# Attention's units 2.05 instead of 1.65 weight blocks apart among the long products of a two-layer hybrid trunk

## The chip, the cores and the metric

The kernel runs on one core of one Trainium2 chip. The metric is the device time of one execution in microseconds, median of the runs. A core has five engines with a queue of instructions each: TensorE (PE in the profile, its weight loads PEld), VectorE (DVE), ScalarE (ACT), GpSimd (POOL) and SyncE (SP, which here only issues transfers). TensorE writes its results to PSUM, of which the kernel uses eight banks of 128 x 512 fp32; VectorE and ScalarE read them out.

## The reference, cut to what matters

Two layers, 512 tokens, model width 1024, fp32. Each layer normalises x, projects it with one wide matrix, runs two branches on parts of the result, merges them under two gates, projects back, and then runs a squared-ReLU MLP of width 4096:

```python
z = rmsnorm(x, norm_mix) @ w_in      # q | k | v | q_m | k_m | v_m | o_m | i/f | gate A | gate B
att = sliding_window_attention(rope(rmsnorm(q)), rope(rmsnorm(k)), v, sinks)   # 8 heads, 2 kv heads of 64
hm  = rmsnorm(mlstm_chunkwise(q_m, k_m, v_m, i, f)) * sigmoid(o_m)             # 4 heads
x = x + (sigmoid(gA) * (att @ w_att_branch) + sigmoid(gB) * (hm @ w_m_branch)) @ w_out
x = x + relu(rmsnorm(x) @ w_ff1)**2 @ w_ff2
```

Attention works on four blocks of 128 queries; each sees its own block and the one before, within 128 positions:

```python
scores = where(valid, q_blk @ [k_prev, k_blk].T / 8, -inf)
m = max(scores.max(-1), sink); p = exp(scores - m)
out = (p / (p.sum(-1) + exp(sink - m))) @ [v_prev, v_blk]
```

## The kernel before, in words

**Products.** Every fp32 weight and activation is split into a high and a low part that TensorE multiplies faster; a product of two split operands is three matmuls (`mm3`). A long product takes weight blocks of 128 x 512: a block is loaded (SP), split by one ScalarE copy (L192) and one VectorE subtraction (L193), and multiplied in four steps of three matmuls each. A step counts as 0.25, so one **weight block** is 1.0 on the scale by which everything here is placed. The results of four steps lie in four PSUM banks until VectorE or ScalarE reads them out (`ev_...`); three pairs of banks, x, y and f, are used in turn by the long products.

**The list of a mixer.** `weave` (L255) takes the steps of the long products in order and a list `side` of other work, each piece with a place on that scale, and emits a piece as soon as the products have reached its place. The products of the second `weave` in a mixer, with the blocks they span: mLSTM q and k 0 to 8, gate products 0 and 1 from 8 to 24, mLSTM v (`ev_v`) 24 to 32, attention's branch product `a_steps` in two halves 32 to 40, gate product 2 to 48, output gate to 56, gate product 3 to 64.

**Emission is not the order on the engines.** The framework orders each engine's instructions once, when the program is built: the earlier an instruction was emitted, the sooner its turn, but one whose inputs, bank or tile are not there yet by its own model of times gives way to later ones that are ready. What stands under `tc.high_priority()` (weight splits, read-outs of the long products) goes ahead. On the chip each engine then works through its fixed order, waiting where something is late. So the profile can show a piece several blocks behind its place.

**Attention, in eight units.** Unit (b, kv) is a block of queries and a kv head, with i = 2 b + kv from 0 to 7. Its steps and what they cost the engines:

- `k_tr(b)` and `q_tr(b)`, once per block: transposes by TensorE into one bank each; k is read out by four ScalarE copies (L593, L594) and four VectorE operations (L595, L596), q by four pairs of a ScalarE copy (L615) and a VectorE operation (L616) that take turns on the bank.
- `att_scores`, twice: matmuls of q with the keys (tile names `aux<-kT,t`) into one bank; ScalarE copies the earlier block's half (L638), VectorE the masked half (L639, `copy_predicated`), which frees the bank.
- `att_softmax`: VectorE maximum (L646, L647), four ScalarE exponentials (L652), VectorE sums and scaling (L655 to L657).
- `att_probs`: four transposes (`aux<-ident,t`), a split by ScalarE (L204) and VectorE (L205), two GpSimd masks (L671, L673).
- `att_out`: two or four matmuls with v (`aux<-t,v`), then ScalarE and VectorE read-outs (L685, L689) and a split (L692, L693) into the tiles that the branch product multiplies.

All these results, and those of the gating and the mLSTM, go through `aux()`, a pool of two PSUM banks. The pool `act` has 24 tiles of 128 x 512 and the pool `tmp` 18.

**Beside attention** stand in the same list `gating0` to `gating3` (small VectorE and ScalarE work for the mLSTM gates, with a few aux matmuls) at 8.45 and every 3 blocks on, and `qk_split` n = 0 to 7 (L709 on), which splits the mLSTM's queries and keys per head: one ScalarE copy (L713), one VectorE subtraction (L718 or L721), for queries a GpSimd copy and memset too. The mLSTM's own heads begin at 28 (`m_decay`), their weights at 29.75.

Places before, in weight blocks: unit i starts at 7 + 1.65 i with its first scores, second scores and softmax 1.25 later, probabilities at + 3.45, output at + 5.65. `q_tr(b+1)` and `k_tr(b+1)` stand 1.75 and 1.25 ahead of the first unit of that block. The splits stand at 9.6 + 1.65 n.

Of the kernel before, what the change touches and what calls it, by code (L numbers as in the profile page):

```python
# [35 lines left out]
def hybrid_kernel(ctx, tc, x, norm_mix, w_in, att_q_norm, att_k_norm, att_sinks, m_gate_bias,  # L36
# [36 lines left out]
    def slot(dt=F32, shape=(P, T)):  # L73
        return now["act"].tile(list(shape), dt, tag="a", name=nm("a"))

    def temp(dt=F32):
        return now["tmp"].tile([P, T], dt, tag="t", name=nm("t"))
# [10 lines left out]
    def aux(shape=(P, T)):  # L88
        return paux.tile(list(shape), F32, tag="aux", name=nm("aux"))
# [4 lines left out]
    def f32(ap):  # L94
        return ap.bitcast(F32)
# [331 lines left out]
    def mixer(l, norm, late, order, phase):  # L427
# [153 lines left out]
        def k_vec(b):  # L581
            rope(kvi[:, b, 0:128].rearrange("p (h d) -> p h d", d=HD), b, HKV)

        def k_tr(b):

            ps = aux([P, P])
            pe.transpose(ps, kvi[:, b, 0:128], ident)
            for h in range(HKV):
                r = slice(64 * h, 64 * h + 64)
                o = slice(64 - 64 * h, 128 - 64 * h)  # L590
                c = slice((b + 1) * P, (b + 2) * P)
                g = gcols[1][r, l:l + 1]
                sc.activation(kTh[r, h, c], ps[r, :], AF.Copy, scale=g)  # L593
                sc.activation(kTh[o, h, c], ps[r, :], AF.Copy, scale=g)  # L594
                ve.scalar_tensor_tensor(kTl[r, h, c], ps[r, :], g, f32(kTh[r, h, c]), op0=ALU.mult, op1=ALU.subtract)  # L595
                ve.tensor_copy(kTl[o, h, c], f32(kTl[r, h, c]))  # L596

        def q_vec(b):
            rope(q_tok[b].rearrange("p (h d) -> p h d", d=HD), b, HQ)

        def q_tr(b):


            ps = aux()
            for j in range(4):
                pe.transpose(ps[:, j * P:(j + 1) * P], q_tok[b][:, j * P:(j + 1) * P], ident)
            for j in range(2):
                qT[b, j] = temp(F32R)
                t4 = qT[b, j].rearrange("p (n i t) -> p n i t", n=2, i=2)
                p4 = ps[:, 2 * j * P:2 * (j + 1) * P].rearrange("p (n t) -> p n t", n=2)  # L610
                for i in range(2):
                    r = slice(64 * i, 64 * i + 64)
                    o = slice(64 - 64 * i, 128 - 64 * i)
                    g = gcols[0][r, l:l + 1]
                    sc.activation(t4[r, :, i, :], p4[r], AF.Copy, scale=g)  # L615
                    ve.scalar_tensor_tensor(t4[o, :, i, :], p4[r], g, f32(t4[r, :, i, :]), op0=ALU.mult,  # L616
                                            op1=ALU.subtract)

        def att_scores(b, kv, hp):
            if hp == 0:  # L620
                sps[b, kv] = temp()
            ps = aux()
            for i in range(2):
                c = 2 * hp + i
                lhs = qT[b, kv][:, c * P:(c + 1) * P]
                o = ps[:, i * 2 * P:(i + 1) * 2 * P]
                ks = slice(b * P, (b + 2) * P)
                if b == 0:

                    o, ks = o[:, P:], slice(P, 2 * P)  # L630
                pe.matmul(o, lhs, kTh[:, kv, ks], start=True, stop=False)
                pe.matmul(o, lhs, kTl[:, kv, ks], start=False, stop=True)
            p4 = ps.rearrange("p (h w k) -> p h w k", h=2, w=2)
            dst = sps[b, kv][:, hp * 2 * P:(hp + 1) * 2 * P].rearrange("p (h k) -> p h k", h=2)
            if b == 0:
                gp.memset(dst, NEG)
            else:
                sc.activation(dst, p4[:, :, 0, :], AF.Copy)  # L638
            ve.copy_predicated(dst, tri_i.unsqueeze(1).to_broadcast([P, 2, P]), p4[:, :, 1, :])  # L639

        def att_softmax(b, kv):
            sp = sps[b, kv]
            s3 = sp.rearrange("p (h k) -> p h k", h=4)
            hs = slice(4 * kv, 4 * kv + 4)
            m = sm([P, 4], "m")
            ve.tensor_reduce(m, s3, axis=AX.X, op=ALU.max)  # L646
            ve.scalar_tensor_tensor(m, m, -1.0, nsinks[:, l, hs], op0=ALU.mult, op1=ALU.min)  # L647
            es = sm([P, 4], "es")
            ve.tensor_tensor(es, sinks[:, l, hs], m, op=ALU.add)
            den = sm([P, 4], "den")  # L650
            for i in range(4):
                sc.activation(s3[:, i, :], s3[:, i, :], AF.Exp, bias=m[:, i:i + 1],  # L652
                              accum_out=den[:, i:i + 1])
            sc.activation(es, es, AF.Exp)
            ve.tensor_tensor(den, den, es, op=ALU.add)  # L655
            ve.reciprocal(den, den)
            ve.tensor_tensor(s3, s3, den.unsqueeze(2).to_broadcast([P, 4, P]), op=ALU.mult)  # L657

        def att_probs(b, kv):
            sp = sps[b, kv]  # L660
            pt = aux()
            for i in range(4):
                pe.transpose(pt[:, i * P:(i + 1) * P], sp[:, i * P:(i + 1) * P], ident)
            hl = split(pt, get=lambda: temp(F32R))
            parts[b, kv] = [(hl, b)]
            if b > 0:

                prev = [temp(F32R) for _ in hl]
                for src, dst in zip(hl, prev):
                    s3, d3 = (t.rearrange("p (h q) -> p h q", h=4) for t in (src, dst))  # L670
                    gp.affine_select(out=d3, in_=s3, compare_op=ALU.is_gt, fill=0.0, base=0,  # L671
                                     pattern=[[0, 4], [-1, P]], channel_multiplier=1)
                    gp.affine_select(out=s3, in_=s3, compare_op=ALU.is_ge, fill=0.0, base=0,  # L673
                                     pattern=[[0, 4], [1, P]], channel_multiplier=-1)
                parts[b, kv].append((prev, b - 1))
# [33 lines left out]
        def qk_split(m, i):  # L709
            t = qk_raw[m]  # L710
            r, o = slice(64 * i, 64 * i + 64), slice(64 - 64 * i, 128 - 64 * i)
            d = slot(F32R)
            sc.activation(d[r], t[r], AF.Copy)  # L713
            if m < 2:
                gp.tensor_copy(d[o], f32(d[r]))
                low = slot(F32R)
                gp.memset(f32(low[o]), 0.0)
                ve.tensor_tensor(low[r], t[r], f32(d[r]), op=ALU.subtract)  # L718
                m_q[2 * m + i], m_ql[2 * m + i] = d, low
            else:  # L720
                ve.tensor_tensor(d[o], t[r], f32(d[r]), op=ALU.subtract)  # L721
                m_k[2 * (m - 2) + i] = d
# [11 lines left out]
        def gate_steps(g, then=lambda: None):  # L734
            sg = []

            def ev(m, ps):
                sg.append(slot())
                ve.tensor_tensor(sg[m], ps, row[0], op=ALU.mult)
                if m == 3:  # L740
                    then()

            return sg, feat_steps(acts, wcols(C_G + 512 * g, 512), ev)
# [3 lines left out]
        def ev_v(b, ps):  # L747
            if b == 0:
# [6 lines left out]
        side = [(0, lambda: k_vec(0)), (0, lambda: q_vec(0)), (0, lambda: k_vec(1)), (0, lambda: q_vec(1)),  # L755
                (7 - 1.25, lambda: k_tr(0)), (7 - 1.75, lambda: q_tr(0))]
        for i, (b, kv) in enumerate(units):
            at = 7 + 1.65 * i
            side += [(at, lambda b=b, kv=kv: att_scores(b, kv, 0)),
                     (at + 1.25, lambda b=b, kv=kv: att_scores(b, kv, 1)),  # L760
                     (at + 1.25, lambda b=b, kv=kv: att_softmax(b, kv)),
                     (at + 3.45, lambda b=b, kv=kv: att_probs(b, kv)),
                     (at + 3.45 + 2.2, lambda b=b, kv=kv: att_out(b, kv))]
            if kv == 0 and b + 1 < NB:
                if b + 2 < NB:
                    side += [(at + 1, lambda b=b: k_vec(b + 2)), (at + 1, lambda b=b: q_vec(b + 2))]
                side += [(at + 2 * 1.65 - 1.25, lambda b=b: k_tr(b + 1)), (at + 2 * 1.65 - 1.75, lambda b=b: q_tr(b + 1))]
        side += [(8.45 + 3.0 * i, f) for i, f in enumerate((gating0, gating1, gating2, gating3))]
        side += [(9.6 + 1.65 * n, lambda n=n: qk_split(n // 2, n % 2)) for n in range(8)]
        g0, s0 = gate_steps(0)  # L770
        g1, s1 = gate_steps(1, lambda: back(sigmoid(g0 + g1)))

# [68 lines left out]
        for h in range(MH):  # L841
            at = 28 + 4.65 * h
# [468 lines left out]
```

## Time and profile before

| | us |
|---|---|
| median of three runs (lowest, highest) | 1323.62 (1322.04, 1324.94) |
| the profiled execution: time, span from first to last instruction | 1324.14, 1322.4 |
| TensorE busy, share of the span | 1296.7, 98% |
| VectorE busy | 953.9, 72% |
| ScalarE busy | 768.4, 58% |
| GpSimd busy | 217.9, 16% |
| second weave of layer 0: first matmul, first of mLSTM v (block 24), first of the branch product (block 32) | 47.72, 132.80, 167.38 |

Times within a trace are counted from the first instruction of the span. A row of the timeline gives start, duration, engine, line, operation, `out<-in` by tile names, partitions and shape, count, and in brackets the idle time of that engine just before it and the instruction that ended it. Matmuls are recorded under L47 and transposes under L51, the lines of the helpers, whatever step they belong to; the tile names tell them apart. Matmuls are pipelined, so their durations overlap.

### The profile page before, as it was taken

How to read it: one execution, taken by the hardware profiler on the slowest of the kernel's cores; microseconds unless marked ns; L12 is line 12 of the kernel's file. 1: busy time of each engine (PE TensorE's matmuls, PEld its weight loads, DVE VectorE, ACT ScalarE, POOL GpSimd, SP SyncE). 2: the span in 40 equal slices, each digit the busy share in tenths (PEclk: the TensorE clock that was granted, in tenths of full speed). 3: DMA queues.
4: the chain of work that ended last, by engine and by line, in shares of the span. 5: the costliest groups of instructions: out<-in, count | busy, mean ns of one | idle time of the engine just before them, and what ended most of it. 6: DMA issues, size and time to landing. Idle time of an engine off the chain costs nothing.

```text
span 1322.4 us, 19224 instructions
## 1 busy us (share of the span) xinstructions
PE 1296.7 (98%) x6966; PEld 1101.0 (83%) x6966; DVE 953.9 (72%) x1493; ACT 768.4 (58%) x1367; POOL 217.9 (16%) x323
## 2 busy tenths in 40 slices
PE   8999999999999999999999999999999999999998
PEld 6877788887889989899788777888888899988987
DVE  4688764466568797978947887645756778879786
ACT  5467765445366655666454687564545566655663
POOL 4422311100001132120005123110000110322100
PEclk9999999999999999999999999999999999999999
DMA  5422236746357989686314222367472589797843
GB/s 152 109 66 75 60 97 153 180 128 218 78 126 187 244 190 236 167 194 194 111 33 120 64 72 64 105 153 174 140 235 66 115 223 251 172 245 149 199 144 128
DMA packets 134400, 192.31 MB, mean 145 GB/s; under 512 B 10264, under 2 KB 71808, under 8 KB 134304
## 3 DMA queue, kind: packets, MB, share of 16 engines
q1 hardware_dynamic: 92768, 135.88, 33.6%
q0 software_dynamic: 33344, 39.98, 19.4%
q10 hardware_dynamic: 8192, 15.21, 3.7%
q8 instruction: 55, 0.90, 0.3%
q14 instruction: 41, 0.34, 0.1%
HBM read 188.95 MB, written 31.46 MB: 167 GB/s over the span
## 4 chain that ended last, share of the span: by engine, by line
PE 48%; DVE 5%; ACT 2%; DMA 2%; issue 1%; DVEq 0%; POOL 0%; SPq 0%; ACTq 0%; POOLq 0%
PE mm L47 42%; PE aux L47 5%; DMA raw<-in_w_ff_dram 1%; PE aux L51 1%; DVE wl L193 1%; DVE wl L911 1%; ACT wh L910 1%; ACT t L652 0%; ACT wh L192 0%; DMA w<-in_w_in_dram 0%; DVE ul L903 0%; DVE x L965 0%; DVE t L639 0%; DVE t L689 0%; DVE t L616 0%
## 5 line engine op out<-in xcount | busy, mean ns | idle before, releaser
L47 PE MATMUL mm<-i,wh 128*128 128x512 f32 (+1 forms) x1280 | 353.6, 362 | 2.2 <-ACT u L1139 2.1
L910 ACT ACTIVATE wh<-raw 128x1024 fp32r<-128x1024 f32 x212 | 223.7, 1056 | 164.5 <-PE mm L47 95.5
L911 DVE TENSOR_TENSOR wl<-raw,wh 128x1024 fp32r<-128x1024 f32 x212 | 257.3, 1220 | 80.1 <-ACT wh L910 79.9
L47 PEld LDWEIGHTS mm<-i,wh 128*128 128x128 f32 x1280 | 224.2, 189 | 36.0 <-ACT u L1139 4.5
L47 PE MATMUL mm<-i,wl 128*128 128x512 f32 (+1 forms) x640 | 230.2, 360 | 0.0
L193 DVE TENSOR_TENSOR wl<-w,wh 128x512 fp32r<-128x512 f32 (+1 forms) x208 | 140.8, 677 | 105.0 <-ACT wh L192 101.2
L192 ACT ACTIVATE wh<-w 128x512 fp32r<-128x512 f32 (+1 forms) x208 | 127.1, 612 | 133.3 <-PE mm L47 99.9
L47 PE MATMUL mm<-wh,ul 128*128 128x512 f32 x448 | 174.8, 390 | 1.1 <-DVE ul L903 1.1
L47 PE MATMUL mm<-wh,uh 128*128 128x512 f32 x448 | 175.1, 391 | 0.0
L47 PE MATMUL mm<-wl,uh 128*128 128x512 f32 x448 | 175.0, 391 | 0.0
L47 PE MATMUL mm<-wh,i 128*128 128x512 f32 (+1 forms) x512 | 149.9, 371 | 0.4 <-ACT wh L192 0.4
L951 POOL DMA_DIRECT2D raw<-in_w_ff_dram x48 | 62.2, 1296 | 522.8 <-DVE wl L911 247.0
L47 PEld LDWEIGHTS mm<-i,wl 128*128 128x128 f32 x640 | 120.9, 189 | 17.6
L47 PE MATMUL mm<-hs,wh 128*128 128x256 f32 x576 | 106.7, 286 | 0.3 <-ACT u L1139 0.3
L47 PEld LDWEIGHTS mm<-wh,i 128*128 128x128 f32 x512 | 92.7, 190 | 16.0 <-ACT wh L192 0.8
L47 PEld LDWEIGHTS mm<-wh,ul 128*128 128x128 f32 x448 | 84.2, 188 | 18.5 <-DVE ul L903 1.6
L47 PEld LDWEIGHTS mm<-wh,uh 128*128 128x128 f32 x448 | 84.3, 188 | 16.4 <-issue 0.2
L47 PEld LDWEIGHTS mm<-wl,uh 128*128 128x128 f32 x448 | 84.3, 188 | 15.7
L47 PEld LDWEIGHTS mm<-hs,wh 128*128 128x128 f32 x576 | 90.1, 191 | 7.5 <-ACT u L1139 6.6
L47 PE MATMUL mm<-wl,i 128*128 128x512 f32 (+1 forms) x256 | 94.8, 370 | 0.0
L965 DVE SCALAR_TENSOR_TENSOR x<-mm,ninv,x 128x512 f32<-128x512 f32 x112 | 80.0, 744 | 16.1 <-PE mm L47 15.6
L47 PE MATMUL mm<-wh,a 128*128 128x512 f32 x256 | 82.1, 394 | 2.3 <-DVE x L879 1.2
(244 smaller groups left out, 2130.5 us busy)
## 6 DMA issues: line engine op xcount, KB each, us to landing
raw<-in_w_ff_dram SPq DMA_DIRECT2D x124, 512.0 KB, 5.1
w<-in_w_in_dram SPq DMA_DIRECT2D x128, 256.0 KB, 2.7
raw<-in_w_ff_dram POOLq DMA_DIRECT2D x48, 512.0 KB, 6.5
sum<-in_w_ff_dram ACTq DMA_DIRECT2D x28, 512.0 KB, 5.0
raw<-sum SPq DMA_DIRECT2D x28, 512.0 KB, 4.2
sum<-in_w_ff_dram POOLq DMA_DIRECT2D x20, 512.0 KB, 6.6
w<-in_w_out_dram SPq DMA_DIRECT2D x32, 256.0 KB, 3.4
w<-in_w_att_branch_dram SPq DMA_DIRECT2D x16, 256.0 KB, 2.6
```

The source lines that it names most:

```text
L47: return nc.tensor.matmul(*args, **kw)
L51: return nc.tensor.transpose(*args)
L192: last_wh[:] = sc.activation(wh[:, :off], raw[:, :off], AF.Copy), wh
L193: ve.tensor_tensor(wl[:, :off], raw[:, :off], f32(wh[:, :off]), op=ALU.subtract)
L910: last_wh[:] = sc.activation(hi, r, AF.Copy), hi[:, 0, :]
L911: ve.tensor_tensor(lo, r, f32(hi), op=ALU.subtract)
L951: nc.gpsimd.dma_start(r, w1_block(k, n, c0), accum_op=ALU.add)
L965: ve.scalar_tensor_tensor(xh[:, i, :], ps[:, i, :], norm.inv[:, 0 if sign > 0 else 1, b:b + 1], xh[:, i, :], op0=ALU.mult, op1=ALU.add)
```

## The change

The distance between units is 2.05 weight blocks instead of 1.65. The constant stands in four places, and all are changed alike: the units, the transpositions of the next block's keys and queries (which keep their 1.25 and 1.75 ahead of that block's first unit), and the distance of the mLSTM's splits. The starts (7 and 9.6), the distances inside a unit, the gating and all else keep their places.

```diff
         for i, (b, kv) in enumerate(units):
-            at = 7 + 1.65 * i
+            at = 7 + 2.05 * i
             side += [(at, lambda b=b, kv=kv: att_scores(b, kv, 0)),
                      (at + 1.25, lambda b=b, kv=kv: att_scores(b, kv, 1)),
                      (at + 1.25, lambda b=b, kv=kv: att_softmax(b, kv)),
...
-                side += [(at + 2 * 1.65 - 1.25, lambda b=b: k_tr(b + 1)), (at + 2 * 1.65 - 1.75, lambda b=b: q_tr(b + 1))]
+                side += [(at + 2 * 2.05 - 1.25, lambda b=b: k_tr(b + 1)), (at + 2 * 2.05 - 1.75, lambda b=b: q_tr(b + 1))]
         side += [(8.45 + 3.0 * i, f) for i, f in enumerate((gating0, gating1, gating2, gating3))]
-        side += [(9.6 + 1.65 * n, lambda n=n: qk_split(n // 2, n % 2)) for n in range(8)]
+        side += [(9.6 + 2.05 * n, lambda n=n: qk_split(n // 2, n % 2)) for n in range(8)]
```

New places: unit i starts at 7 + 2.05 i, so the units stand at 7, 9.05, 11.1, 13.15, 15.2, 17.25, 19.3 and 21.35 instead of 7, 8.65, 10.3, 11.95, 13.6, 15.25, 16.9 and 18.55; the last output stands at 27.0 instead of 24.2, the last split at 23.95 instead of 21.15.

## The prediction

> **What bounds the kernel now.** I read the page first (busy shares), then the granted clock and busy time of each stretch of the two mixers, then what TensorE waited for there, then the timeline around its longest wait.
>
> ```profile
> span 1322.4 us, 19224 instructions
> PE 1296.7 (98%) x6966; PEld 1101.0 (83%) x6966; DVE 953.9 (72%) x1493; ACT 768.4 (58%) x1367; POOL 217.9 (16%) x323
> ```
>
> TensorE (PE) is busy for all but 1322.4 - 1296.7 = 25.7 us, and the change neither adds nor removes a matmul. So whatever it is worth comes out of idle time of PE, or is added to it. The stretch it touches is the mixer of each layer, from the mLSTM q/k product (block 0 of the long list of products) to the first branch product (block 32). One line per stretch, columns: window, length, busy us and count of PE, PEld, DVE, ACT, POOL, then granted clock, DMA share, GB/s. The first four are layer 0, the last four layer 1.
>
> ```profile
> 68.00:90.00 22.00, 19.97 (x109) 16.20 (x110) 18.91 (x51) 13.72 (x39) 6.35 (x13) 1.00 0.27 72
> 90.00:111.00 21.00, 20.39 (x100) 15.91 (x99) 17.23 (x40) 16.18 (x39) 0.00 (x0) 1.00 0.29 76
> 111.00:132.80 21.80, 20.86 (x99) 15.86 (x97) 19.44 (x45) 16.45 (x44) 6.68 (x8) 1.00 0.28 72
> 132.80:167.40 34.60, 33.94 (x163) 26.41 (x162) 26.13 (x68) 26.54 (x75) 10.61 (x17) 1.00 0.20 61
> ...
> 723.00:745.00 22.00, 20.00 (x111) 16.22 (x110) 18.93 (x51) 13.75 (x39) 6.39 (x13) 1.00 0.27 71
> 745.00:766.00 21.00, 20.38 (x99) 15.90 (x98) 17.21 (x40) 16.16 (x39) 0.00 (x0) 1.00 0.27 76
> 766.00:787.80 21.80, 20.91 (x98) 15.87 (x97) 19.44 (x44) 16.46 (x44) 6.68 (x8) 1.00 0.27 73
> 787.80:822.40 34.60, 33.87 (x163) 26.37 (x162) 26.17 (x68) 26.53 (x75) 10.61 (x17) 1.00 0.20 60
> ```
>
> The clock is 1.00 throughout. PE idles 2.03 + 0.61 + 0.94 + 0.66 = 4.24 us in layer 0 and 2.00 + 0.62 + 0.89 + 0.73 = 4.24 us in layer 1: the two layers wait at the same places for the same times, so a term found in one counts twice. VectorE (DVE) is the fullest helper: 18.91/22.00 = 86%, then 82%, 89%, 76%.
>
> What PE waited for in layer 0 (total, times, longest), and the longest wait in both layers:
>
> ```profile
> PE aux L51 <- DVE t L639: 2.2, 3, 1.5
> PE aux L47 <- DVE t L689: 0.7, 1, 0.7
> PE aux L47 <- DVE t L639: 0.5, 1, 0.5
> PE aux L51 <- DVE t L689: 0.3, 1, 0.3
> ...
> 80.15 0.39 PE L47 MATMUL mm<-i,wh 128*128 128x512 f32 x1
> 82.07 0.30 PE L51 MATMUL aux<-ident,kvi 128*128 128x128 f32 x1 [1.53 <-DVE t L639]
> 84.91 0.79 PE L47 MATMUL aux<-kT,t 128*128 128x256 f32 x4 [0.48 <-DVE t L639]
> ...
> 737.07 0.30 PE L51 MATMUL aux<-ident,kvi 128*128 128x128 f32 x1 [1.52 <-DVE t L639]
> 739.92 0.35 PE L47 MATMUL aux<-kT,t 128*128 128x256 f32 x1 [0.47 <-DVE t L639]
> ```
>
> All six named waits (3.7 us a layer) are for an `aux` bank: attention's small matmuls share two PSUM banks, and a third user waits until DVE has emptied one. The first, k_tr(1) at 82.07, is the largest single term: 1.53 us idle. A wait costs a little more than its idle time: the matmul at 80.15 is modelled 0.39 us long, while its neighbours start 0.23 us apart, so about 0.16 us of pipelining is lost with each.
>
> **Why that wait is there.** At 73.79 q_tr(1) takes one bank, at 74.14 the first scores of unit (0,1) take the other:
>
> ```profile
> 73.79 0.60 PE L51 MATMUL aux<-ident,a 128*128 128x128 f32 x4
> 74.14 0.64 PE L47 MATMUL aux<-kT,t 128*128 128x128 f32 x4
> ...
> 74.43 0.47 ACT L615 ACTIVATE t<-aux,gc 64x256 fp32r<-64x256 f32 x1 [0.67 <-PE aux L51]
> 75.97 0.40 ACT L652 ACTIVATE t<-t,m 128x128 f32<-128x128 f32 x1 [0.42 <-DVE m L647]
> 78.26 0.47 ACT L615 ACTIVATE t<-aux,gc 64x256 fp32r<-64x256 f32 x1
> 81.48 0.47 ACT L615 ACTIVATE t<-aux,gc 64x256 fp32r<-64x256 f32 x1 [0.77 <-DVE t L616]
> ...
> 81.48 0.44 DVE L639 COPY_PREDICATED t<-tri_l,aux 128x256 f32<-128x256 int32 x1
> 81.98 0.49 DVE L616 SCALAR_TENSOR_TENSOR t<-aux,gc,t 64x256 fp32r<-64x256 f32 x1
> ```
>
> ScalarE (ACT) starts q_tr(1)'s first copy at 74.43, then the softmax of unit (0,0) comes in between (75.97 on), and the last of the four copies ends at 81.95. DVE empties the score bank only at 81.48 to 81.92, behind that chain. Both banks are thus held for about 8 us, and k_tr(1), whose turn by the list is right after, finds none.
>
> **The change, part by part.** No operation is added or removed, nothing changes shape, no DMA is issued by the moved steps themselves; the list is only sorted differently.
>
> Units: unit i's five steps move later by 0.4 i blocks (unit 7 by 2.8). For units 1 to 3 that bites. From 47.72 (block 0) to 132.80 (block 24) a block takes 85.08/24 = 3.54 us, so unit 4's first scores, below at 106.03, run at about block 16.5. The new list asks for them at 7 + 4 x 2.05 = 15.2. Unit 7's, at 145.64, run about (145.64 - 132.80)/((167.38 - 132.80)/8) = 3.0 blocks behind block 24, at 27.0; the new list asks for 21.35. Late units are held up by the engines and the banks already, not by their place, so for units 4 to 7 I put the move at nothing by itself. If that cover is gone, the cost is the tail, below.
>
> ```profile
> 47.72 0.39 PE L47 MATMUL mm<-i,wh 128*128 128x512 f32 x1
> ...
> 106.03 0.35 PE L47 MATMUL aux<-kT,t 128*128 128x256 f32 x1
> ...
> 132.80 0.40 PE L47 MATMUL mm<-wh,i 128*128 128x512 f32 x1
> ...
> 145.64 0.28 PE L47 MATMUL aux<-kT,t 128*128 128x256 f32 x1
> ```
>
> Transpositions: q_tr(1) goes from 8.55 to 9.35, k_tr(1) from 9.05 to 9.85, and the first scores of unit (0,1) from 8.65 to 9.05. So these scores now come ahead of q_tr(1), not behind it, and DVE can empty their bank (0.44 us) before q_tr(1)'s copies queue up. Then k_tr(1) has a bank when its turn comes: gain 1.53 + 0.16 = 1.69 us a layer. The next wait, 0.48 + 0.16 = 0.64 us at 84.91 (first scores of unit (1,0), list place 10.3 before and 11.1 after), sits 0.8 blocks later behind the same copies; I count it gone too. Together 2.33 us a layer.
>
> What is late next: q_tr(1) still needs four ACT copies and four DVE operations in turn, 4 x (0.47 + 0.49) = 3.8 us at least and 8 us as the trace has it, on one of the two banks, and starts 0.8 blocks later. Whoever follows k_tr(1), the second scores of unit (0,1) at 10.3, may now find both banks held by q_tr(1) and k_tr(1). That new wait is between nothing (q_tr(1) meets an ACT whose softmax is done) and the old 1.69 us (the same jam, one step later). No row shows it; I take the middle, 0.85 us a layer, as nothing in the rows sets the one end nearer.
>
> [...]
>
> mLSTM's splits: qk_split 0 stays at 9.6, the eighth goes from 21.15 to 23.95. Their groups (us in all, mean ns) in the stretch:
>
> ```profile
> L713 ACT ACTIVATE a<-a 64x512 fp32r<-64x512 f32 x8 | 5.0, 627 | 0.1
> L721 DVE TENSOR_TENSOR a<-a,a 64x512 fp32r<-64x512 f32 x4 | 3.4, 851 | 0.1
> ```
>
> None of them feeds PE before the mLSTM weights at block 29.75: more than five blocks, some 20 us, cover even the last. The second gate product's four results at block 24 want slots: of 24, the queries hold 4, the splits' results 12, the first gate's 4, and the two key tiles not yet split through 2, so two results find room at once, and these are the two whose bank the V product takes next. Cost nothing; with that cover gone, one subtraction, 0.85 us.
>
> Order against the rest: with 2.05 instead of 1.65, about 5.65/2.05 = 2.8 units are open at once, not 3.4, and probabilities and outputs of unit i come ahead of the scores of units i+2 and i+3. The remaining idle time, 4.24 - 2.01 = 2.23 us a layer, will be dealt anew; bounds plus or minus 1.5 us a layer (all but 0.7 gone, or as much again added), value nothing.
>
> Sum: 2 x (2.33 - 0.85) = 3.0 us off. The profiled execution took 1324.14 us (span 1322.4 and 1.7 around it), so 1321.1; it lay 0.5 above the median of the runs, 1323.62, and against that the forecast is 1320.6.
>
> **The rivals.** (1) *The wait only moves.* The model by which the instructions were ordered evidently puts q_tr(1)'s end 1.5 us too early; PE runs into it with whichever step is next in line, now the scores at 10.3. For it: DVE at 86% where the wait is, two banks only. Against it: the scores at 9.05 no longer sit behind the copies. Time: 1323.62 plus or minus 1.5.
>
> (2) *Attention's tail reaches the first branch product: slower.* That product reads all blocks' outputs of kv 0. Its first matmul is at 167.38; the last piece it needs, from unit (3,0), ends at 161.92 + 0.57 = 162.49:
>
> ```profile
> 158.75 0.47 PE L47 MATMUL aux<-t,v 128*128 128x512 f32 x1
> ...
> 161.92 0.57 DVE L693 TENSOR_TENSOR u<-t,u 128x128 fp32r<-128x128 f32 x2 [0.38 <-ACT u L692]
> ...
> 167.38 0.61 PE L47 MATMUL mm<-u,wh 128*128 128x512 f32 x2
> ```
>
> The slack is 4.9 us. Unit 6's place moves by 2.4 blocks, at 4.3 us each there 10.4 us. Its output matmuls, at 158.75, run about (158.75 - 132.80)/4.3 = 6 blocks behind block 24, at 30 against a listed 22.55. If that lag stayed as it is, PE would wait 10.4 - 4.9 = 5.5 us a layer, 11 in all; if half the delay comes through, 5.2 - 4.9 = 0.3. It decides from 47% of the delay coming through. Three quarters, 2.9 us a layer, gives 1323.62 + 5.8 = 1329.4, less the forecast's 3.0: 1326.4. Against it: units 4 to 7 run behind even the new places, so little should come through; for it: DVE at 76 to 89% cannot make up much.
>
> (3) *The jam dissolves altogether*: idle of both layers 8.5 us and 12 named waits x 0.16 = 1.9, 10.4 off; with three quarters of it removed, 7.8: 1315.8.
>
> **How the numbers follow.** Forecast 0.41, wait only moves 0.24, tail 0.25, dissolves 0.10. A measurement of this kernel can tell about 0.2%, 2.6 us, from no change, so the bounds are 1321.0 and 1326.3. The forecast's 1320.6 lies close to the first: its own range, 1317 to 1323.6 (new wait nothing or 1.69 us, and some of the re-dealt idle), puts 0.29 of its 0.41 below the bound and 0.12 within. Of the moved wait 0.03 falls below, 0.16 within, 0.05 above; of the tail 0.05 within, 0.20 above; the third is all faster. Faster 0.42, same 0.33, slower 0.25. The range: 1314.0, where the third rival is nearly whole, to 1328.5, where the tail's 5.8 us come with little of the gain; it leaves out the tail at its full 11 us.
>
> **What would show it.** Right: the k_tr(1) matmul (aux from kvi, second of its kind in each layer) without idle time ahead of it, PE's idle in the 22 us from 68 on about 1 us instead of 2, V's first matmul at about 131.3 instead of 132.80. Rival 1: the 1.5 us stand in front of a scores matmul or of q_tr instead. Rival 2: PE idle in front of the first branch product, ended by L693 or L692. Wrong altogether would be idle time that appears outside blocks 7 to 34 of the mixer, in the MLP, or in unlike places in the two layers.

## The result, and the profile after

The change makes the kernel slower: 1327.17 us against 1323.62, medians of 21 runs each; ratio 1.0025, 95% interval 1.0019 to 1.0031. The profiled execution took 1327.17 us, its span 1325.4. The forecast was 3 us faster. The time is inside the stated range, on its far side, but that is luck: the upper end was set by the tail of the second rival, which did not come.

Two lines of the page, then the second weave of each layer up to block 24 and from there to the branch product (columns as in the prediction: window, length, busy us and count of PE, PEld, DVE, ACT, POOL, granted clock, DMA share, GB/s). The kernel before:

```profile
47.72:132.80 85.08, 81.36 (x395) 63.98 (x393) 71.25 (x171) 57.35 (x145) 26.79 (x53) 1.00 0.30 81
132.80:167.38 34.58, 33.92 (x163) 26.39 (x162) 26.13 (x68) 26.52 (x75) 10.61 (x17) 1.00 0.20 61
703.43:787.81 84.38, 80.86 (x394) 64.03 (x393) 70.64 (x170) 56.50 (x144) 26.90 (x53) 1.00 0.30 82
787.81:822.39 34.58, 33.84 (x162) 26.37 (x161) 26.16 (x68) 26.51 (x75) 10.61 (x17) 1.00 0.20 60
```

The changed kernel, with the 3.4 us behind its longest wait in the last line:

```profile
span 1325.4 us, 19222 instructions
PE 1298.4 (98%) x6966; PEld 1102.6 (83%) x6966; DVE 956.8 (72%) x1493; ACT 768.2 (58%) x1367; POOL 221.3 (17%) x323
...
47.70:136.57 88.87, 84.96 (x411) 67.45 (x410) 75.45 (x182) 60.02 (x151) 28.75 (x55) 0.98 0.29 78
136.57:169.15 32.58, 31.65 (x147) 24.41 (x145) 24.22 (x57) 24.00 (x70) 10.52 (x17) 1.00 0.20 62
705.10:792.45 87.35, 83.36 (x411) 66.09 (x409) 75.09 (x181) 59.28 (x150) 28.73 (x55) 1.00 0.29 79
792.45:825.36 32.91, 31.96 (x147) 24.37 (x146) 24.22 (x57) 24.12 (x70) 10.59 (x17) 1.00 0.21 61
83.90:87.30 3.40, 3.40 (x14) 3.03 (x13) 2.56 (x7) 1.18 (x4) 0.00 (x0) 0.50 0.28 77
```

From block 0 to 32, layer 0 takes 121.45 us instead of 119.66, layer 1 120.26 instead of 118.96: together 3.1 more, which is the 3.0 by which the span grew. Some 16 small matmuls of attention have come ahead of block 24 (411 instead of 395), so the stretch behind it is shorter; that part is a shift. PE's idle time goes from 4.38 and 4.26 us to 4.84 and 4.94, 1.1 us in all. And one thing is new in the mixers: a stretch of 3.4 us in layer 0 in which the granted clock is 0.50.

The timeline of PE around it, and the same wait in layer 1:

```profile
78.09 0.27 PE L51 MATMUL aux<-ident,kvi 128*128 128x128 f32 x1
...
80.72 0.39 PE L47 MATMUL mm<-i,wl 128*128 128x512 f32 x1
80.94 0.39 PE L47 MATMUL mm<-i,wh 128*128 128x512 f32 x1
83.39 0.64 PE L47 MATMUL aux<-kT,t 128*128 128x128 f32 x4 [2.06 <-DVE kT L595]
83.97 1.11 PE L51 MATMUL aux<-ident,t 128*128 128x128 f32 x4
84.73 0.78 PE L47 MATMUL mm<-i,wh 128*128 128x512 f32 x1
85.31 0.63 PE L47 MATMUL mm<-i,wl 128*128 128x512 f32 x1
85.73 1.05 PE L47 MATMUL aux<-kT,t 128*128 128x256 f32 x4
...
740.33 0.41 PE L47 MATMUL aux<-kT,t 128*128 128x128 f32 x2 [2.03 <-DVE kT L595]
```

k_tr(1) at 78.09 no longer waits. But the second scores of unit (0,1), at 83.39, wait 2.06 us in one piece, where before 1.53 and 0.48 us were waited apart. Half a microsecond later, at 83.90, the granted clock is 0.50: a matmul of 512 columns starts 0.42 us after the one before it (85.31 to 85.73) instead of 0.22 (80.72 to 80.94). At about 0.43 instead of 0.23 us a matmul, 3.41 us of it lose, by estimate, 3.41 x (1 - 0.23/0.43) = 1.6 us. In layer 1 the same wait of 2.03 us passes without it (1.00 from 705.10 to 792.45).

How often the half clock comes can be read from the mean granted clock of each execution. Profiles without it in the mixers have a mean of 0.999 or 1.000 (the end of the span may cost 0.001: the last 2.5 us of the changed kernel's have 0.51), the two with one such stretch 0.998, those with two 0.997 and the one with three 0.996. Of the 21 executions of the changed kernel six have 0.999 or 1.000 and take 1325.6 us on average, eight have 0.998 and take 1326.6, seven have 0.997 or less and take 1329.0. Of 60 executions of the kernel before, 59 have 0.999 or 1.000. So the half clock came, by estimate, in about 15 of 21; without it the changed kernel is still about 2 us slower.

Why the second scores wait: both transposes are read out at the same time. ScalarE and VectorE in that stretch:

```profile
76.95 0.40 ACT L652 ACTIVATE t<-t,m 128x128 f32<-128x128 f32 x1 [1.20 <-DVE m L647]
...
78.51 0.19 ACT L654 ACTIVATE es<-es 128x4 f32<-128x4 f32 x1
78.72 0.47 ACT L615 ACTIVATE t<-aux,gc 64x256 fp32r<-64x256 f32 x1
79.62 0.35 ACT L593 ACTIVATE kT<-aux,gc 64x128 fp32r<-64x128 f32 x1
...
82.88 0.47 ACT L615 ACTIVATE t<-aux,gc 64x256 fp32r<-64x256 f32 x1
...
77.51 0.44 DVE L639 COPY_PREDICATED t<-tri_l,aux 128x256 f32<-128x256 int32 x1
82.89 0.36 DVE L595 SCALAR_TENSOR_TENSOR kT<-aux,gc,kT 64x128 fp32r<-64x128 f32 x1 [0.28 <-ACT kT L594]
83.42 0.49 DVE L616 SCALAR_TENSOR_TENSOR t<-aux,gc,t 64x256 fp32r<-64x256 f32 x1
```

The first scores' bank is emptied from 77.51 to 77.95, as foreseen, and k_tr(1) takes it at 78.09. q_tr(1) has held the other bank since 76.27, but ScalarE comes to it only at 78.72, behind the softmax of unit (0,0) (L652, L654). From then on q_tr(1)'s reads (L615, L616) and k_tr(1)'s (L593 to L595) alternate on both engines, so neither bank comes free until 82.89 + 0.36 = 83.25 (k_tr(1)) and 83.42 + 0.49 = 83.91 (q_tr(1)). PE is there at 81.2.

### The profile page after: what moved, and what is told of

Read it like the earlier page. It is cut to its first block, busy times and chain, and to the rows that moved or that the text cites. A ratio compares the mean times of both kernels' runs of the same rounds, so it can differ in the third digit from the quotient of the medians.

```text
span 1325.4 us, 19222 instructions
## 1 busy us (share of the span) xinstructions
PE 1298.4 (98%) x6966; PEld 1102.6 (83%) x6966; DVE 956.8 (72%) x1493; ACT 768.2 (58%) x1367; POOL 221.3 (17%) x323
## 3 DMA queue, kind: packets, MB, share of 16 engines
q0 software_dynamic: 33344, 39.98, 19.3%
## 4 chain that ended last, share of the span: by engine, by line
PE 48%; DVE 4%; DMA 2%; ACT 2%; issue 1%; POOL 0%; DVEq 0%; SPq 0%; ACTq 0%; POOLq 0%
PE mm L47 42%; PE aux L47 5%; DMA raw<-in_w_ff_dram 1%; PE aux L51 1%; DVE wl L911 1%; DVE wl L193 1%; ACT wh L910 1%; DMA w<-in_w_in_dram 0%; DVE ul L903 0%; ACT wh L192 0%; DVE x L965 0%; DVE a L721 0%; DVE t L689 0%; DVE t L205 0%; DVE a L869 0%
```

## The experiments

Each time is a median of 5 to 12 executions (one each in the two repeats), followed by the ratio to the kernel before, run beside it, and its 95% interval; the profile is of one execution.

Theory A: the loss is that one wait, made by the first block's moves, and the half clock that a wait so long lets in. Rival B: the order is dealt anew all along, and the loss lies in the later units. Rival C: the splits.

**The splits back.**

```diff
-        side += [(9.6 + 2.05 * n, lambda n=n: qk_split(n // 2, n % 2)) for n in range(8)]
+        side += [(9.6 + 1.65 * n, lambda n=n: qk_split(n // 2, n % 2)) for n in range(8)]
```

> The changed kernel with the eight mLSTM splits back at 9.6 + 1.65 n. Theory A (the loss is the wait in front of the second scores of unit (0,1), where k_tr(1) and q_tr(1) hold both banks, 2.06 us in one piece, plus a stretch of half clock that such a wait lets in): the splits have no part in it, 1326.5 to 1328, that wait still about 2 us in both layers. Rival C (the splits' later places make VectorE and ScalarE late): back to 1323.6, within 1.3.

1328.13 us (1.0036, 1.0023 to 1.0048), 0.1 above A's range. Rival C falls. The wait is the same, and here the half clock is in layer 1:

```profile
82.71 0.30 PE L47 MATMUL aux<-kT,t 128*128 128x128 f32 x1 [2.03 <-DVE kT L595]
740.21 0.30 PE L47 MATMUL aux<-kT,t 128*128 128x128 f32 x1 [2.06 <-DVE kT L595]
...
83.00:86.40 3.40, 3.13 (x22) 2.47 (x20) 3.13 (x8) 1.76 (x6) 0.00 (x0) 1.00 0.28 77
741.04:744.45 3.41, 3.41 (x13) 2.85 (x12) 2.80 (x7) 1.60 (x6) 0.00 (x0) 0.50 0.30 77
```

**Only the first block's moves, on the kernel before.**

```diff
-            at = 7 + 1.65 * i
+            at = 9.05 if i == 1 else 7 + 1.65 * i
...
+                nxt = 11.1 if b == 0 else at + 2 * 1.65
-                side += [(at + 2 * 1.65 - 1.25, lambda b=b: k_tr(b + 1)), (at + 2 * 1.65 - 1.75, lambda b=b: q_tr(b + 1))]
+                side += [(nxt - 1.25, lambda b=b: k_tr(b + 1)), (nxt - 1.75, lambda b=b: q_tr(b + 1))]
```

> The kernel before with only unit (0,1) at 9.05 and q_tr(1), k_tr(1) at 9.35 and 9.85, as the change has them; all later units, transpositions and the splits stay. Theory A: the wait of about 2 us in front of the second scores of unit (0,1) is there in both layers, time 1326 to 1328. Rival B (the loss comes from the later units and the order dealt anew behind block 12): no more than 1324.5.

1329.38 us (1.0039, 1.0026 to 1.0051), above the range that A gave. Unit (0,1) 0.4 blocks later and two transpositions 0.8 later are enough for the whole loss; the two waits are there, and after the first the half clock lasts two stretches:

```profile
82.81 0.30 PE L47 MATMUL aux<-kT,t 128*128 128x128 f32 x1 [2.03 <-DVE kT L595]
740.83 0.30 PE L47 MATMUL aux<-kT,t 128*128 128x128 f32 x1 [2.06 <-DVE kT L595]
...
84.59:91.42 6.83, 6.74 (x29) 5.81 (x30) 3.91 (x23) 2.63 (x12) 0.00 (x0) 0.50 0.15 38
```

**Only the first block's moves undone, in the changed kernel** (the mirror image: unit (0,1) at 8.65, q_tr(1) at 8.55, k_tr(1) at 9.05; all else 2.05 apart).

> The changed kernel with only unit (0,1), q_tr(1) and k_tr(1) back at 8.65, 8.55 and 9.05; all else 2.05 apart. Theory A: no wait of 2 us in one piece, clock 1.000, time at most 1324.5. Rival B: 1326 or more, with waits behind block 12.

1332.54 us (1.0070, 1.0058 to 1.0083): A's number is far off, and B's "1326 or more" holds. The 2 us wait in front of the second scores is gone, as A says, and the 1.53 of before is back. What A did not have is a new place, in both layers, just ahead of the branch product:

```profile
166.74 0.50 PE L47 MATMUL aux<-t,v 128*128 128x512 f32 x1 [1.92 <-POOL t L673]
168.17 0.80 PE L47 MATMUL aux<-t,v 128*128 128x512 f32 x1 [0.92 <-POOL t L673]
170.04 0.63 PE L47 MATMUL mm<-u,wh 128*128 128x512 f32 x1
...
826.28 0.51 PE L47 MATMUL aux<-t,v 128*128 128x512 f32 x1 [1.92 <-POOL t L673]
...
168.06:171.47 3.41, 3.30 (x8) 2.63 (x9) 0.84 (x2) 1.44 (x3) 0.06 (x1) 0.50 0.00 0
826.83:833.66 6.83, 5.96 (x15) 4.85 (x16) 3.07 (x11) 3.74 (x11) 1.36 (x3) 0.50 0.01 4
```

Attention's last output waits for the mask of its probabilities (L673 on GpSimd). The V product ahead of it has ended and the branch product stands behind it, so PE has nothing else to run: the place of the prediction's second rival, though that rival named L692 or L693 as what would end the wait, in a kernel where it was not looked for, and again with half clock behind it. So the loss does not lie in one place whatever the rest does: B has its share. Each order has its own collisions.

**More work for PE ahead of the wait.** Eight matmuls whose result nothing uses:

```diff
+        def keep_busy():
+            two = banks("f")
+            for _ in range(8):
+                pe.matmul(two[:, 0, :], acts[0][0][:, 0:P], acts[0][0], start=True, stop=True)
+
+        side += [(10.29, keep_busy)]
```

> The changed kernel with eight matmuls of 128x512 (about 1.8 us) on a free PSUM bank put in the list just ahead of the second scores of unit (0,1), in both layers; their result is used by nothing. Theory A: they run in time in which TensorE waited, so its wait there falls from 2.06 us to about 0.3, the span pays little or nothing for them, and the clock does not fall: 1.000, and no more than 1326, some 1.5 below the changed kernel. If instead the clock falls in some executions whatever TensorE does there, or the wait is no free time: 1327 to 1331.

1327.70 us (1.0035, 1.0023 to 1.0047): inconclusive. The wait did not shrink as expected, 1.83 and 1.81 us: the planner saw the extra work too and moved seven matmuls of the product behind the scores. Between k_tr(1) and the scores stand 14 matmuls (eight of them the new ones) instead of 13, so PE came to the bank only 0.2 us later. The profile has no half clock, but this execution was the fastest of its six (1326.17 to 1330.07); the mean clock is 1.000 in three of them (1326.17, 1326.94, 1328.45) and 0.997 or 0.998 in the other three.

**Hold back what asks for the bank.** The pieces with places between 10.2 and 11.9 go to 11.9, in their order:

```diff
+        held, until = 10.2, 11.9
+        side = [(until if held < p < until else p, f) for p, f in sorted(side, key=lambda e: e[0])]
```

> The changed kernel with every piece whose place lies between 10.2 and 11.9 (second scores and softmax of unit (0,1), probabilities of (0,0), first scores of (1,0), gating1, one split, two rope steps) put at 11.9, so that TensorE has about 11 more matmuls of the long product before it asks for the bank of k_tr(1). Theory A (wait of 2.06 us in one piece and the half clock it lets in make the loss): no wait of 1 us or more there, clock 1.000, 2 x 2.2 us of waiting and one to two stretches of half clock (1.7 us each) less than 1327.2: 1320.5 to 1323. Rival B (order dealt anew; the wait only moves on to the next piece again): 1325.5 to 1329, a wait of 1 us or more right behind.

1321.90 us (0.9984, 0.9975 to 0.9992), within A's range. The scores find the bank free; what is left there is 1.00 us in front of the next piece:

```profile
83.04 0.56 PE L47 MATMUL aux<-kT,t 128*128 128x128 f32 x4
...
85.29 0.71 PE L47 MATMUL aux<-kT,t 128*128 128x256 f32 x4 [1.00 <-DVE t L639]
...
46.69:131.70 85.01, 81.38 (x403) 64.95 (x402) 72.24 (x177) 58.99 (x149) 26.89 (x53) 1.00 0.30 81
701.73:785.96 84.23, 81.07 (x402) 65.07 (x401) 72.00 (x176) 58.13 (x148) 26.83 (x53) 1.00 0.30 81
```

The mean clock is 0.999 or 1.000 in all eleven executions. This version beats both kernels, the one before by 2.1 us (median of the 29 executions run beside it, 1323.96).

**The same cure for the kernel before** (`held, until = 9.0, 11.5`).

> The kernel before with every piece whose place lies between 9.0 and 11.5 (k_tr(1), second scores and softmax of unit (0,1), first scores of (1,0), probabilities of (0,0), gating1, two splits, two rope steps) put at 11.5. Theory A: its 1.53 and 0.48 us of waiting in each layer go, 2 x 2.3 us: 1319 to 1321. Rival B: within 1.5 of 1323.6 or above, with waits behind block 12 longer by what was saved.

1322.73 us (0.9991, 0.9983 to 1.0000). Its 1.53 us wait goes and PE's idle in the two weaves falls from 8.6 to 6.4 us, but the time by some 1 us only, and so does PE's idle time over the whole span (25.7 to 24.6 us); the expected 1319 to 1321 is missed, and the time lies within rival B's range. Compared like with like, both kernels with pieces held back, the distance of 2.05 is worth 0.8 us (1321.90 against 1322.73), with intervals that overlap.

**Read-outs of the transposes first** (`with tc.high_priority():` around them), in the changed kernel and in the one before.

> The changed kernel with the read-outs of k_tr and q_tr (copies on ScalarE, subtractions on VectorE) under high priority, so that they go ahead of splits, softmax and long products' read-outs that are ready at the same time. Theory A: the banks are held shorter, and the wait in front of the second scores of unit (0,1) shrinks from 2.06 to at most 1 us in both layers; 1322 to 1325. Rival B: the order is planned by the same model of times, which still thinks the banks free too early; wait 1.5 to 2.1 us as before, 1326 to 1329.

> The same high priority in the kernel before. Theory A: its 1.53 us wait in front of k_tr(1) shrinks to at most 0.8; 1320 to 1323. Rival B: 1322.5 to 1327, the wait as long or moved.

1330.20 us (1.0050, 1.0039 to 1.0062) and 1323.60 (0.9996, 0.9988 to 1.0005). The waits stay:

```profile
83.58 0.39 PE L47 MATMUL aux<-kT,t 128*128 128x128 f32 x1 [2.11 <-DVE kT L596]
...
83.64:87.05 3.41, 3.41 (x15) 3.20 (x16) 3.14 (x7) 1.40 (x3) 0.00 (x0) 0.50 0.38 112
742.41:745.82 3.41, 3.06 (x11) 2.71 (x11) 2.05 (x6) 2.05 (x10) 0.00 (x0) 0.50 0.33 82
```

(the second kernel's wait in front of k_tr(1) is 1.57 us). That is what rival B said of the waits, though 1330.20 lies above its range too. In the second kernel the bank is emptied sooner, but k_tr(1) is planned sooner as well (117 matmuls of the product stand ahead of it instead of 130), and the chip is late by as much. In the first the priority changed little: the softmax still goes ahead of the read-outs, and k_tr(1)'s bank is held 5.4 us instead of 5.2.

**Half the cure** (`held, until = 10.2, 11.3`).

> The changed kernel with the pieces between 10.2 and 11.3 put at 11.3: TensorE runs some five matmuls of the long product more (1.1 us) before it asks for k_tr(1)'s bank, so the wait there should shrink from 2.06 to about 0.9 us in both layers, not go. If the clock's part is real and needs a long wait: no half clock, 2 x 1.1 of waiting and about 2 us of half clock less: 1322.5 to 1323.8. If only the waiting counts and the half clock comes anyway: 1324.5 to 1326.

1322.62 us (0.9990, 0.9981 to 0.9998). The waits are 0.91 and 0.95 us, and the profile has no half clock in the mixers. The time comes out where the half clock was counted in, but the test is not as sharp as it looked. Four of its eleven executions have a mean clock of 0.997 or 0.998 and take 1323.5 us on average, the other seven 0.999 or 1.000 and 1321.9: the half clock came in some, and what waits those had is not known. Besides, layer 1 of the changed kernel, which had no half clock in its profile, takes 120.26 us and here 118.16, 2.1 us less where the wait shrank by 1.1.

**The changed kernel twice more**, for its clock.

> The changed kernel again, unaltered, for its clock. If the half clock follows a wait of 2 us by chance of when it falls: the two waits of 2.0 to 2.1 us are there as before, each followed within 2 us by a stretch of half clock of 3.4 us (or two of them) or by none, and the span is near 1323.8 plus 1.65 for each stretch.

> As the run before it: the same two waits, none, one or more stretches of half clock behind them, a span of 1323.8 plus 1.65 for each. If the span is unlike that by over 0.8 us, something else varies between executions.

1327.73 and 1330.17 us, spans 1326.0 and 1328.5. Both have the same two waits (2.02 and 2.06; 2.04 and 2.07 us) and two stretches of half clock, one in each layer in the first, both in layer 1 in the second:

```profile
84.97:88.38 3.41, 3.41 (x12) 3.00 (x12) 1.69 (x5) 1.91 (x9) 0.00 (x0) 0.50 0.28 77
740.33:743.74 3.41, 3.41 (x13) 2.98 (x14) 2.74 (x6) 1.26 (x5) 0.00 (x0) 0.50 0.29 77
```

```profile
85.00:88.40 3.40, 3.13 (x22) 2.47 (x20) 3.13 (x8) 1.76 (x6) 0.00 (x0) 1.00 0.29 77
742.90:749.70 6.80, 6.80 (x28) 5.66 (x28) 3.39 (x20) 2.67 (x11) 0.00 (x0) 0.50 0.16 41
```

The spans miss the expected 1327.1 by -1.1 and +1.4 us, so something else varies too. The second weave of layer 0 begins at 46.47 and 47.67 here, at 47.70 in the first profile, and a wait near its beginning is 0.82 and 1.33 us here and 0.01 there: together most of the second miss and some of the first.

**A distance between the two.** 1.85 in all four places.

> The changed kernel with 1.85 in all four places. Theory A (what counts is which piece meets a held bank, not the distance): anything from 1321 to 1330, with waits at places of their own; where there is a wait of 1.9 us or more in one piece, half clock behind it in some executions. Rival B' (wider spacing is worse in itself): between the two, 1324.5 to 1326.

1324.67 us (1.0011, 1.0002 to 1.0021), just within the range of "wider is worse" and within that of A, so it does not part them. Its wait at that place is 1.32 us; the mean clock is 0.999 or 1.000 in all ten executions, the profiled one (0.999) among them.

## Why the prediction was wrong, point by point

- **What bounds the kernel** was read rightly: PE's work is fixed, and all that moved is its idle time and its clock in the two mixers. That a term of one layer counts twice held for the waits (2.06 and 2.03 us), not for the clock, which fell in one layer only in the first profile.
- **The transpositions.** k_tr(1) lost its 1.53 us wait and the wait of 0.48 in front of unit (1,0) went (0 us is left in layer 0, 0.26 in layer 1), so nearly all of the 2.33 us a layer was won, and paid again at the next place. The mechanism was the foreseen one: L639 came at 77.51 instead of 81.48.
- **What is late next** is the step that failed. The place was named, the second scores of unit (0,1), but its price was bounded at the top by the old wait, 1.69 us with its pipelining, and put at 0.85. It is 2.06 idle and 2.2 with it. The bound left out that k_tr(1), now admitted, is read out alternately with q_tr(1), so that each holds its bank longer. The rows for it were at hand: four L593 and L594 copies of 0.36 us to be added to the four of L615. The low end, an ACT that is done with its softmax, did not come either: q_tr(1) waited for that from 76.27 to 78.72. With the real price the sum would have been 2 x 2.33 - (2.22 + 2.19) = 0.25 us faster instead of 3.0, that is, no change; what makes the kernel slower than that stands mainly in the next two points.
- **The clock** had no term at all. The row with 1.00 was taken as given, when it was read in a kernel with no wait longer than 1.53 us. Taking 0.998 as one stretch, 0.997 as two and so on, the 21 executions had about 1.2 each; at 1.6 us, an estimate of 1.9 us.
- **The other idle time, dealt anew at a value of nothing,** grew by about 0.8 us in both layers together (1.1 in all, less 0.3 by which the waits named above grew), within the bounds of 1.5 us a layer.
- **Units 4 to 7 at nothing** held for the tail here: PE does not wait in front of the branch product at 169.15, the slack there is 5.3 us (unit (3,0)'s last piece ends at 163.89) instead of 4.9, and the second rival did not come. Not all of them kept their time, though: unit 4's first scores came at 115.09 instead of 106.03. In the kernel with the first block's moves undone, a small change of order brought in a wait at the tail.
- **Splits at nothing** held: without their move 1328.1 against 1327.2, the intervals overlapping.
- **The rivals.** The first, that the wait only moves, is what happened, at the place it named, but its time, plus or minus 1.5 us about the old one, was too low, for want of the clock. The 0.25 given to slower lay almost all with the tail, which did not come. Against the forecast of 1320.6 the median is 6.6 us too high: 2.7 of it are the new waits' price, 0.3 the wait left in front of unit (1,0) in layer 1, 0.8 the other idle time and about 1.9 the clock; the remaining 0.9 are not assigned. In the three profiled executions of the changed kernel, 3.0, 3.6 and 6.1 us longer in span than the one of the kernel before, PE's idle time over the whole span is 1.3, 1.5 and 2.7 us more, and the rest is longer busy time, with one, two and two stretches of half clock. The waits at the beginning of the weave, which vary from execution to execution, are part of that idle time.

## What to carry to other kernels

When a fixed order makes an engine wait for a buffer, moving one user out of the way admits the next: price the new holder's own time in the buffer, with the reads of both holders counted together, before calling the old wait a ceiling. Neither higher priority for the reads nor more work ahead helped here: the planner moved other pieces along, or left the order much as it was. What helped was holding back the pieces that ask for the buffer. And two short waits need not cost the same as one of their sum: behind those of 1.53 and 0.48 us in the kernel before the granted clock stayed at 1.00, behind the one of 2.06 us in the changed kernel it was 0.50 for 3.4 us. Look at the longest single gap of the tensor engine, and at the granted clock of every execution, as well as at the total.

## What the runs showed that was not expected

In these runs the half clock came behind long single waits, and behind only some of them. In the fourteen profiles, leaving aside the start and the end of the span, a granted clock of 0.50 appears nowhere but within 2.3 us behind a wait of 1.92 us or more: 14 such waits (twelve of 2.02 to 2.11 us, and the two of 1.92 that a second of 0.92 follows), of which 10 had it, seven for 3.40 or 3.41 us and three for 6.80 or 6.83. Behind the two waits of 1.81 and 1.83 us and behind those of 1.6 us and less there was none in these profiles; of the executions of which only the mean clock is kept, four with the short hold and three with the eight extra matmuls have 0.997 or 0.998.

The length of a wait does not tell which ones were hit. Behind 2.03 us in layer 0 the clock was 1.00 with the splits back and 0.50 with only the first block's moves; behind 2.06 us in layer 1 it was the other way round, 0.50 and, in this row, 1.00:

```profile
741.00:747.00 6.00, 5.90 (x44) 4.81 (x43) 5.34 (x25) 3.84 (x14) 0.00 (x0) 1.00 0.18 46
```

What decides it, and why three of the ten lasted twice as long, is open.
